# MLP down products with the activations stationary, and the MLP's split weights in other pools

## The chip, the cores and the metric

The kernel runs on one core of one Trainium2 chip. The metric is the device time of one execution in microseconds; runs of a kernel are compared by their median. A core has TensorE (PE in the profile; its weight loads are listed as PEld), VectorE (DVE), ScalarE (ACT), GpSimd (POOL) and SyncE (SP), which here issues all DMAs. "Granted clock" is the share of TensorE's full clock that the throttle allowed.

## The reference

One sequence of 256 tokens, width 2048, two layers. The first is an RWKV-7 layer, the second a forgetting-attention layer; after each stands the same MLP:

```python
def squared_relu_mlp(h, w_up, w_down):
    return jnp.square(jax.nn.relu(h @ w_up)) @ w_down
...
        x = x + mixed
        x = x + squared_relu_mlp(rms_norm(x, ffn_norm[layer]), mlp_w_up[layer], mlp_w_down[layer])
    return rms_norm(x, final_norm)
```

`w_up` is 2048 x 8192 and `w_down` 8192 x 2048 in each layer, all in float32: 64 MB each, 256 MB for both layers. All weights of the model are read once from HBM.

## The kernel before, in words

**Layout.** The stream `xT` lies in SBUF turned: 128 partitions hold 128 of the 2048 channels, 16 k-tiles, 256 tokens along the free side. An operand of a product (`opA`, `opB`) has for each k-tile two 256-column halves: a high part rounded to the type fp32r, and the rest, the low part. A weight block is treated in the same way: `load_split` (line 194 on) loads a raw block (tile `wr`, line 196), ScalarE casts it to the high part `wh` (line 204), and VectorE subtracts to get the low part `wl` (line 206). A product is high x high + high x low + low x high, three terms in fp32r. The other big products of the kernel (`gemm_steps`, line 216 on, matmuls in lines 212 to 214) do this with three 256-column matmuls for each 128x128 weight block; they load 256 rows x 512 columns at a time (512 KB) into the pool `wraw` (four buffers) and split k-tile by k-tile into `wsp` (five).

**The MLP before.** The hidden width of 8192 is taken in 4 chunks c of 2048. For each chunk come 4 up groups g of 512 columns, whose results become the operand `b`, and then 4 down groups of 512 columns. Both use `gemm_wide` (line 241 on). For each of 16 k-tiles and 4 weight blocks m of 128 columns, with the weight block stationary, there is one 512-column matmul, high weights against both halves of the activations (line 254), and one 256-column matmul, low weights against the high half (line 256). So lengths alternate: 512, 256, 512, 256. Each of the four m has one PSUM bank, [128, 512]; successive products take turns between the pool `psm` (4 banks, tag "mm") and the pool `pss` (4 banks, tag "side"), by the counter `wide`. At the end of a group ScalarE copies one half of each bank (line 261), VectorE adds the other (line 262), and `evac` goes on from there: for an up group relu (351), square on GpSimd (353) and the split into `b` (342, 343); for a down group the scaling by the norm's factor `r2` on VectorE (363) and the addition to `xT` on GpSimd (366, the last group of a layer on VectorE). Because relu and square let a positive factor through, the MLP's norm is not applied to its operand: `r2`, 1/mean-square by token, scales the down products. It is made after the first up group (`norm.ln`, line 324 with four matmuls against a matrix of ones, then two activations).

Loads are 512 rows x 512 columns (1024 KB, `WK` = 4 k-tiles) in three raw buffers of the MLP's own (`mraw0`, `mraw1`), splits are of two k-tiles at a time in three buffers each (`msp0`, `msp1`). In layer 0 the pools are opened in the order raw, split, other tiles; in layer 1 other tiles, raw, split.

**Around it.** Ahead of the MLP of layer 0 the last quarter of the time-mixing output projection runs (`gemm_group` with `w_o`), whose results are added to x (line 846) and at once scaled and split into the MLP's operand (lines 337 and 338). It uses two banks of `psm` per group. After the last chunk's down group, `final` is called for each pair of k-tiles: in layer 0 it makes squares for the next norm and the operand of the key/value product, in layer 1 squares for the final norm (306, 312) and the scaling by the final gain (1026); then come the final norm and the output DMAs. After layer 0's MLP come the forget-gate product (tile `zp`, in the pool `pss`), the key product (`gemm_steps`) and the value product, lines 920 to 931. The value product is written the other way round: the activations are stationary, 128 tokens at a time, and 512 columns of split weights are streamed (lines 929 to 931, tile `mmv`), so that its result lies with the tokens on the partitions; lines 932 and 933 scale it by token.

**Order.** The kernel is written in the Tile framework, whose scheduler places the instructions on each engine's queue, mostly in the order of the code, but not always: a few MLP matmuls, splits and loads stand in the queues among those of the projection before it. Each engine, and SP's queue of DMAs, goes through its queue in order. A tile with `bufs=n` takes n buffers in turn, and an instruction that writes a buffer waits until the last reader of its earlier content is through.

Of the kernel before, what the change touches and what calls it, by code (L numbers as in the profile page):

```python
# [10 lines left out]
F32 = mybir.dt.float32  # L11
F32R = mybir.dt.float32r
F16 = mybir.dt.float16
AF = mybir.ActivationFunctionType
ALU = mybir.AluOpType
# [3 lines left out]
P = 128  # L19
T = 256  # L20
D = 2048
# [7 lines left out]
RMS_EPS = 1e-6  # L29
CDEC = math.exp(-0.5)  # L30
NEG = -1.0e30
WK, WRAW, WSP = 4, 3, 3

VEC = ["mix0", "mix1", "ffn0", "ffn1", "fin", "kvn", "xm0", "xm1", "xm2", "xm3", "xm4", "xm5",
       "w0", "a0", "kk", "ka", "rk", "lnw", "lnb"]
# [84 lines left out]
def trunk_kernel(ctx: ExitStack, tc: tile.TileContext, xin, vecs, bfv, c32, c16, w_rkv, w1, w2, a1, a2, g1, g2,  # L120
# [64 lines left out]
    def side(name):  # L185
        return pss.tile([P, 512], F32, tag="side", name=name)

    def bcast(ap, n):
        return ap[:, None, :].to_broadcast([ap.shape[0], n, ap.shape[1]])
# [46 lines left out]
            for b in range(2):  # L236
                evac(b, ps[b])

    wide = {"n": 0}

    def gemm_wide(w, col, x, name, pool, wpools, evac):


        wide["n"] += 1
        ps = [(psm if wide["n"] % 2 else pss).tile([P, 512], F32, tag="mm" if wide["n"] % 2 else "side", name="mmw")
              for _ in range(4)]
        for k0 in range(0, KT, WK):
            hl = load_split(w[k0 * P:(k0 + WK) * P, col:col + 512].rearrange("(k p) n -> p k n", p=P), P, WK, 512, 2,
                            *wpools)
            for kk in range(WK):  # L250
                k = k0 + kk
                h, lo = hl[kk]
                for m in range(4):
                    mm(ps[m], h[:, m * P:(m + 1) * P], x[:, k].rearrange("p h t -> p (h t)"), start=k == 0, stop=False,  # L254
                       skip_group_check=True)
                    mm(ps[m][:, 0:T], lo[:, m * P:(m + 1) * P], x[:, k, 0, :], start=False, stop=k == KT - 1,  # L256
                       skip_group_check=True)
        for b in range(2):
            t = pool.tile([P, 2, T], F32, tag=name, name=name, bufs=3)
            for j in range(2):  # L260
                nc.scalar.copy(t[:, j, :], ps[2 * b + j][:, T:2 * T])
                V.tensor_tensor(t[:, j, :], ps[2 * b + j][:, 0:T], t[:, j, :], op=ALU.add)
            evac(b, t)
# [80 lines left out]


    def mlp(layer, norm, pool, wpools, a, b, final):
        r2 = None
        for c in range(FF // D):
            for g in range(4):
                def up_evac(i, t, g=g):  # L350
                    act(t, t, AF.Relu)  # L351
                    s = pool.tile([P, 2, T], F32, tag="ms", name="ms", bufs=3)
                    G.tensor_tensor(s, t, t, op=ALU.mult)  # L353
                    k = 4 * g + 2 * i
                    split(s, b[:, k:k + 2, 0, :], b[:, k:k + 2, 1, :])
                gemm_wide(w_up[layer], c * D + g * 512, a, "mt", pool, wpools, up_evac)
                if r2 is None:
                    norm.ln()
                    r2 = norm.power(-1.0, "nr2")
            for g in range(4):  # L360
                def down_evac(i, t, g=g, c=c):
                    k = 4 * g + 2 * i
                    V.tensor_tensor(t, t, bcast(r2, 2), op=ALU.mult)  # L363
                    xs = xT[:, k:k + 2, :]
                    end = c == FF // D - 1
                    (V if end and g == 3 else G).tensor_tensor(xs, xs, t, op=ALU.add)  # L366
                    if end:
                        final(2 * g + i)
                gemm_wide(w_down[layer, c * D:(c + 1) * D, :], g * 512, b, "mt", pool, wpools, down_evac)


    HA, HB = slice(0, 64), slice(64, 128)
# [493 lines left out]
    def after0(kp):  # L866
        norm2.add(kp)
        operand("kvn", kp, opBH, opBL)
    with tc.tile_pool(name="mraw0", bufs=WRAW, reuse_waits="tile") as mr, \
            tc.tile_pool(name="msp0", bufs=WSP, reuse_waits="tile") as ms, \  # L870
            tc.tile_pool(name="mlp0", bufs=2, reuse_waits="tile") as mp:
        for g in range(4):
            gemm_group(w_o, 512 * g, opAH, opAL, o_evac_for(g), range(12, 16), po[g] if g < 2 else None)
        mlp(0, norm, mp, (mr, ms), opB, opA, after0)


    s_c = dpool.tile([HEADS, T], F32, name="s_c")
# [138 lines left out]


    norm4 = Norm(npool, "n3")
    with tc.tile_pool(name="mlp1", bufs=2, reuse_waits="tile") as mp, \
            tc.tile_pool(name="mraw1", bufs=WRAW, reuse_waits="tile") as mr, \  # L1020
            tc.tile_pool(name="msp1", bufs=WSP, reuse_waits="tile") as ms:

        def after1(kp):
            norm4.add(kp, kp >= KT // 2 - 2)
            for k in (2 * kp, 2 * kp + 1):
                act(xT[:, k, :], xT[:, k, :], AF.Copy, scale=vcol("fin", k))
        mlp(1, norm3, mp, (mr, ms), opA, opB, after1)
        norm4.ln()
        rf = norm4.power(-0.5, "nrf")
        osrc = out.rearrange("(k p) t -> p k t", p=P)  # L1030
        for kp in range(KT // 2):
            xs = xT[:, 2 * kp:2 * kp + 2, :]
            (G if kp in (1, 5) else V).tensor_tensor(xs, xs, bcast(rf, 2), op=ALU.mult)
            dma(osrc[:, 2 * kp:2 * kp + 2, :], xs)
# [53 lines left out]
```

## Time and profile before

| | |
|---|---|
| time, median of 3 runs | 2511.7 us (2502.09, 2511.7, 2518.87) |
| the profiled execution's own time | 2515.21 us |
| its span, first to last instruction | 2513.4 us |
| mean granted clock | 0.993 |
| TensorE, VectorE, ScalarE, GpSimd busy | 98%, 63%, 51%, 13% |
| DMA queue, share of 16 engines | 57.1% |
| read from HBM, written | 445.44 MB, 24.13 MB, 187 GB/s over the span |
| MLP of layer 0, first to last matmul of tile mmw | 649.6 to 1383.8 us |
| MLP of layer 1 | 1783.7 to 2495.1 us |

How to read the lines below. A group of instructions is given as: line, engine, operation, output tile <- input tiles, shapes, count | busy us, mean ns of one | idle time of the engine before them and what ended it. A row by stretches of time has: the stretch, its length, then for PE, PEld, DVE, ACT and POOL the busy time and in brackets the number of instructions (where the view is of one line alone, only the engines that the line uses), then granted clock, mean share of the DMA engines, GB/s. A row by time has the start, the duration, engine, line, operation and, in square brackets, the wait before it and who ended it. A row by tile has the shortest, median and longest duration in ns and the first and last start. A row by waits has who waited for whom, total us, times, longest. Matmuls are pipelined: their durations overlap, and the distance between starts is what one costs.

### The profile page before, as it was taken

What the parts mean: (1) busy time and instruction counts of PE and PEld (TensorE: products, weight loads), DVE (VectorE), ACT (ScalarE), POOL (GpSimd) and SP (SyncE); (2) the same over time, 40 slices, a digit from 0 to 9 for tenths busy, and PEclk for the clock granted to TensorE, in tenths of its full rate; (3) what the DMA queues carried; (4) which work ended last, traced back from release to release, by engine and by line L of the source; (5) the groups of instructions that cost most, each with busy time, mean ns of one, the idle gap of its engine ahead of it and who ended that gap; (6) DMA issues with size and microseconds to landing.
All of it is one profiled execution on the core that took longest, in us unless ns stands there. A gap on an engine that the chain in (4) does not pass through costs nothing.

```text
span 2513.4 us, 49132 instructions
## 1 busy us (share of the span) xinstructions
PE 2454.1 (98%) x20214; PEld 2198.8 (87%) x20214; DVE 1592.7 (63%) x2329; ACT 1270.8 (51%) x2072; POOL 325.2 (13%) x272
## 2 busy tenths in 40 slices
PE   7999999999999999999999999999999999999997
PEld 6999988789888888888888998999988888888886
DVE  7986677766755555555557655677555555555555
ACT  3866545454554454444445444555454454544554
POOL 1000001001311112112112100110112102112112
PEclk9999999999999999999999999999999999999998
DMA  5777865554755555555553456546355555655653
GB/s 162 237 247 244 266 206 161 180 169 152 262 188 185 185 185 187 187 190 188 179 192 135 149 185 193 174 164 228 131 185 189 195 187 188 194 188 187 195 188 118
DMA packets 274017, 472.76 MB, mean 188 GB/s; under 512 B 43248, under 2 KB 53760, under 8 KB 273792
## 3 DMA queue, kind: packets, MB, share of 16 engines
q1 hardware_dynamic: 273792, 469.62, 57.1%
q8 instruction: 158, 2.59, 0.4%
q14 instruction: 67, 0.55, 0.1%
HBM read 445.44 MB, written 24.13 MB: 187 GB/s over the span
## 4 chain that ended last, share of the span: by engine, by line
PE 90%; DVE 5%; DMA 3%; ACT 1%; issue 1%; DVEq 0%; SPq 0%; ACTq 0%
PE mmw L254 38%; PE mmw L256 19%; PE mm L212 7%; PE mm L214 7%; PE mm L213 7%; PE zyus L778 1%; PE i L609 1%; PE mmv L929 1%; PE mmv L930 1%; PE mmv L931 1%; DVE wl L206 1%; PE lps L473 1%; DMA k<-s_k 1%; DMA wr<-in_mlp_w_up_dram 1%; PE mmg L508 1%
## 5 line engine op out<-in xcount | busy, mean ns | idle before, releaser
L206 DVE TENSOR_TENSOR wl<-wr,wh 128x1024 fp32r<-128x1024 f32 (+1 forms) x1013 | 975.7, 967 | 747.0 <-ACT wh L204 740.2
L204 ACT CAST wh<-wr 128x512 fp32r<-128x512 f32 (+1 forms) x1011 | 841.4, 837 | 910.3 <-PE mmw L254 594.9
L254 PE MATMUL mmw<-opB,wh 128*128 128x512 f32 x2048 | 717.4, 396 | 5.1 <-DVE xT L846 5.1
L254 PE MATMUL mmw<-opA,wh 128*128 128x512 f32 x2048 | 718.0, 396 | 0.2 <-ACT wh L204 0.2
L256 PE MATMUL mmw<-opA,wl 128*128 128x256 f32 x2048 | 571.6, 279 | 0.9 <-DVE wl L206 0.9
L256 PE MATMUL mmw<-opB,wl 128*128 128x256 f32 x2048 | 570.8, 279 | 0.0
L254 PEld LDWEIGHTS mmw<-opB,wh 128*128 128x128 f32 x2048 | 384.4, 188 | 97.7 <-DVE xT L846 5.3
L254 PEld LDWEIGHTS mmw<-opA,wh 128*128 128x128 f32 x2048 | 384.4, 188 | 93.3 <-ACT wh L204 0.5
L256 PEld LDWEIGHTS mmw<-opA,wl 128*128 128x128 f32 x2048 | 385.7, 188 | 1.4 <-DVE wl L206 1.3
L256 PEld LDWEIGHTS mmw<-opB,wl 128*128 128x128 f32 x2048 | 385.6, 188 | 0.2
L212 PE MATMUL mm<-opB,wh 128*128 128x256 f32 x1024 | 298.7, 293 | 0.4 <-ACT opB L342 0.3
L213 PE MATMUL mm<-opB,wh 128*128 128x256 f32 x1024 | 292.9, 286 | 1.5 <-DVE opB L343 0.7
L214 PE MATMUL mm<-opB,wl 128*128 128x256 f32 x1024 | 291.9, 286 | 1.6 <-DVE wl L206 1.6
L212 PE MATMUL mm<-opA,wh 128*128 128x256 f32 x768 | 227.1, 296 | 0.2 <-ACT wh L204 0.2
L214 PE MATMUL mm<-opA,wl 128*128 128x256 f32 x768 | 218.3, 284 | 0.6 <-DVE wl L206 0.5
L213 PE MATMUL mm<-opA,wh 128*128 128x256 f32 x768 | 217.9, 284 | 0.0
L213 PEld LDWEIGHTS mm<-opB,wh 128*128 128x128 f32 x1024 | 197.1, 193 | 4.9 <-DVE opB L343 2.0
L212 PEld LDWEIGHTS mm<-opB,wh 128*128 128x128 f32 x1024 | 196.5, 192 | 5.5 <-ACT opB L342 2.1
L214 PEld LDWEIGHTS mm<-opB,wl 128*128 128x128 f32 x1024 | 196.7, 192 | 2.9 <-DVE wl L206 2.1
L366 POOL TENSOR_TENSOR xT<-xT,mt 128x512 f32<-128x512 f32 x60 | 128.8, 2146 | 533.8 <-DVE mt L363 533.8
L353 POOL TENSOR_TENSOR ms<-mt 128x512 f32<-128x512 f32 x64 | 81.1, 1267 | 636.5 <-ACT mt L351 636.5
L212 PEld LDWEIGHTS mm<-opA,wh 128*128 128x128 f32 x768 | 147.5, 192 | 3.1 <-ACT wh L204 0.4
(259 smaller groups left out, 2499.9 us busy)
## 6 DMA issues: line engine op xcount, KB each, us to landing
wr<-in_mlp_w_up_dram SPq DMA_DIRECT2D x128, 1024.0 KB, 5.4
wr<-in_mlp_w_down_dram SPq DMA_DIRECT2D x128, 1024.0 KB, 5.0
wr<-in_w_rkv_dram SPq DMA_DIRECT2D x96, 512.0 KB, 4.7
wr<-in_w_kvf_dram SPq DMA_DIRECT2D x64, 512.0 KB, 3.6
wr<-in_w_o_dram SPq DMA_DIRECT2D x32, 512.0 KB, 4.1
wr<-in_fox_w_q_dram SPq DMA_DIRECT2D x32, 512.0 KB, 3.5
wr<-in_fox_w_o_dram SPq DMA_DIRECT2D x32, 512.0 KB, 3.8
wr<-in_g_dram SPq DMA_DIRECT2D x8, 512.0 KB, 4.1
```

Of the source, the lines that this page charges most:

```text
L204: nc.scalar.copy(h, raw[:, k:k + per, :])
L206: (G if share["l"] and c % share["l"] == 0 else V).tensor_tensor(lo, raw[:, k:k + per, :], h.bitcast(F32), op=ALU.subtract)
L212: mm(ps, wh, xh, start=first and bank_first, stop=False, skip_group_check=True)
L213: mm(ps, wh, xl, start=False, stop=False, skip_group_check=True)
L214: mm(ps, wl, xh, start=False, stop=last, skip_group_check=True)
L254: mm(ps[m], h[:, m * P:(m + 1) * P], x[:, k].rearrange("p h t -> p (h t)"), start=k == 0, stop=False, skip_group_check=True)
L256: mm(ps[m][:, 0:T], lo[:, m * P:(m + 1) * P], x[:, k, 0, :], start=False, stop=k == KT - 1, skip_group_check=True)
L353: G.tensor_tensor(s, t, t, op=ALU.mult)
L366: (V if end and g == 3 else G).tensor_tensor(xs, xs, t, op=ALU.add)
L473: mm(ps[0:c1 - c0, m, :], raw[:, kk, c0:c1], xs, start=k == 0 and m == 0, stop=k == KT - 1, skip_group_check=True)
L508: mm(ps[:, m, :], raw[:, kk, c:c + P], gh[:, kk, :], start=kk == 0 and m == 0, stop=kk == 1, skip_group_check=True)
L609: mm(ps[hs, c, :], lhs[hs, c, :], rhs[hs, c, :] if len(rhs.shape) == 3 else rhs[hs], start=start, stop=True, skip_group_check=True)
```

## The change

- `WK` goes from 4 to 2 (loads of 512 KB), the MLP's own raw pools go, and the loads use `wraw`, the pool of the other products. `WSP` goes from 3 to 4. The split pool is opened first, the pool of the other tiles after it, in both layers.
- The up products stay in `gemm_wide`; for two k-tiles there are now eight 512-column matmuls, then eight 256-column ones. The counter `wide` begins at 1, so that the first product takes `pss`.
- The down products go to the new `down_group`: the activations are stationary (128 tokens i, high or low part), 512 columns of split weights are streamed, three matmuls for each k-tile and i. The result lies with the tokens on the partitions, in one bank for each i. It is scaled by token (`rc`) and gathered over the four chunks in an SBUF tile `y` [128, 2, 2048]: the first chunk by ScalarE, the others by one VectorE pass each. For the last two k-tiles all of i = 0 comes before i = 1.
- In the last chunk `finish(g)` turns `y` back: eight 128x128 transposes on TensorE in two tiles `ytp`, and VectorE adds them to `xT`; then `final`. It is called for group g after the first two k-tiles of group g + 1, for the last group at the end.
- `norm.ln` comes after the second up group, and after the fourth `r2` is turned into the column `rc` by two transposes and a copy.

```diff
-WK, WRAW, WSP = 4, 3, 3
+WK, WSP = 2, 4
...
-    wide = {"n": 0}
+    wide = {"n": 1}
...
-            for kk in range(WK):
-                k = k0 + kk
-                h, lo = hl[kk]
-                for m in range(4):
-                    mm(ps[m], h[:, m * P:(m + 1) * P], x[:, k].rearrange("p h t -> p (h t)"), start=k == 0, stop=False,
-                       skip_group_check=True)
-                    mm(ps[m][:, 0:T], lo[:, m * P:(m + 1) * P], x[:, k, 0, :], start=False, stop=k == KT - 1,
-                       skip_group_check=True)
+            for k1 in range(0, WK, 2):
+                ks = [(k0 + k1 + i, *hl[k1 + i]) for i in range(2)]
+                for k, h, _ in ks:
+                    for m in range(4):
+                        mm(ps[m], h[:, m * P:(m + 1) * P], x[:, k].rearrange("p h t -> p (h t)"), start=k == 0,
+                           stop=False, skip_group_check=True)
+                for k, _, lo in ks:
+                    for m in range(4):
+                        mm(ps[m][:, 0:T], lo[:, m * P:(m + 1) * P], x[:, k, 0, :], start=False, stop=k == KT - 1,
+                           skip_group_check=True)
...
     def mlp(layer, norm, pool, wpools, a, b, final):
-        r2 = None
+        y = pool.tile([P, 2, D], F32, tag="y", name="y", bufs=1)
+        late = []
+
+        def down_group(c, g):
+
+            pool_, tag = ((pss, "side"), (psm, "mm"))[g // 2]
+            ps = [pool_.tile([P, 512], F32, tag=tag, name="mmd") for _ in range(2)]
+            for k0 in range(0, KT, WK):
+                r0 = c * D + k0 * P
+                hl = load_split(w_down[layer, r0:r0 + WK * P, g * 512:g * 512 + 512]
+                                .rearrange("(k p) n -> p k n", p=P), P, WK, 512, 2, *wpools)
+                last = k0 + WK == KT
+                for i, kk in [(i, kk) for i in range(2) for kk in range(WK)] if last else \
+                        [(i, kk) for kk in range(WK) for i in range(2)]:
+                    k, t = k0 + kk, slice(i * P, (i + 1) * P)
+                    h, lo = hl[kk]
+                    mm(ps[i], b[:, k, 0, t], h, start=k == 0, stop=False)
+                    mm(ps[i], b[:, k, 1, t], h, start=False, stop=False)
+                    mm(ps[i], b[:, k, 0, t], lo, start=False, stop=k == KT - 1)
+                    if last and kk == WK - 1:
+                        yg = y[:, i, g * 512:g * 512 + 512]
+                        if c == 0:
+                            act(yg, ps[i], AF.Copy, scale=rc[:, i:i + 1])
+                        else:
+                            V.scalar_tensor_tensor(yg, ps[i], rc[:, i:i + 1], yg, op0=ALU.mult, op1=ALU.add)
+                if k0 == 0 and late:
+                    finish(late.pop())
+
+        def finish(g):
+
+            for j in range(2):
+                kp = 2 * g + j
+                tp = side("ytp").rearrange("p (k t) -> p k t", k=2)
+                for kk in range(2):
+                    for i in range(2):
+                        n = (2 * kp + kk) * P
+                        nc.tensor.transpose(tp[:, kk, i * P:(i + 1) * P], y[:, i, n:n + P], C("ident"))
+                xs = xT[:, 2 * kp:2 * kp + 2, :]
+                V.tensor_tensor(xs, tp, xs, op=ALU.add)
+                final(kp)
+
...
-                if r2 is None:
+                if c == 0 and g == 1:
                     norm.ln()
                     r2 = norm.power(-1.0, "nr2")
+                if c == 0 and g == 3:
+                    rps = side("rc")
+                    for i in range(2):
+                        nc.tensor.transpose(rps[:, i * P:(i + 1) * P], r2[:, i * P:(i + 1) * P], C("ident"))
+                    rc = pool.tile([P, 2], F32, tag="rc", name="rc", bufs=1)
+                    V.tensor_copy(rc, rps.rearrange("p (i n) -> p i n", n=P)[:, 0:2, 0])
             for g in range(4):
-                def down_evac(i, t, g=g, c=c):
-                    k = 4 * g + 2 * i
-                    V.tensor_tensor(t, t, bcast(r2, 2), op=ALU.mult)
-                    xs = xT[:, k:k + 2, :]
-                    end = c == FF // D - 1
-                    (V if end and g == 3 else G).tensor_tensor(xs, xs, t, op=ALU.add)
-                    if end:
-                        final(2 * g + i)
-                gemm_wide(w_down[layer, c * D:(c + 1) * D, :], g * 512, b, "mt", pool, wpools, down_evac)
+                down_group(c, g)
+                if c == FF // D - 1:
+                    late.append(g)
+        finish(late.pop())
...
-    with tc.tile_pool(name="mraw0", bufs=WRAW, reuse_waits="tile") as mr, \
-            tc.tile_pool(name="msp0", bufs=WSP, reuse_waits="tile") as ms, \
+    with tc.tile_pool(name="msp0", bufs=WSP, reuse_waits="tile") as ms, \
             tc.tile_pool(name="mlp0", bufs=2, reuse_waits="tile") as mp:
...
-        mlp(0, norm, mp, (mr, ms), opB, opA, after0)
+        mlp(0, norm, mp, (wraw, ms), opB, opA, after0)
...
-    with tc.tile_pool(name="mlp1", bufs=2, reuse_waits="tile") as mp, \
-            tc.tile_pool(name="mraw1", bufs=WRAW, reuse_waits="tile") as mr, \
-            tc.tile_pool(name="msp1", bufs=WSP, reuse_waits="tile") as ms:
+    with tc.tile_pool(name="msp1", bufs=WSP, reuse_waits="tile") as ms, \
+            tc.tile_pool(name="mlp1", bufs=2, reuse_waits="tile") as mp:
...
-        mlp(1, norm3, mp, (mr, ms), opA, opB, after1)
+        mlp(1, norm3, mp, (wraw, ms), opA, opB, after1)
```

## The prediction

> **What bounds the kernel now.** I read first the page: busy times, the chain that ended last, the costliest groups.
>
> ```profile
> PE 2454.1 (98%) x20214; PEld 2198.8 (87%) x20214; DVE 1592.7 (63%) x2329; ACT 1270.8 (51%) x2072; POOL 325.2 (13%) x272
> PE 90%; DVE 5%; DMA 3%; ACT 1%; issue 1%; DVEq 0%; SPq 0%; ACTq 0%
> L254 PE MATMUL mmw<-opB,wh 128*128 128x512 f32 x2048 | 717.4, 396 | 5.1 <-DVE xT L846 5.1
> L256 PE MATMUL mmw<-opA,wl 128*128 128x256 f32 x2048 | 571.6, 279 | 0.9 <-DVE wl L206 0.9
> ```
>
> TensorE ends 90% of the chain, and the wide products of the two MLPs (tile mmw, two lines, 4096 matmuls each) are most of it. The 396 and 279 ns are latencies that overlap; what counts is the distance from one start to the next. For that I took stretches in which TensorE never waits and divided their length by the matmuls in them: the two MLPs, the key product (256 columns only) and the value product (512 columns only, activations stationary, the form that the change gives the down products), with the instructions of all engines, and then line 254 alone.
>
> ```profile
> 1415.00:1480.00 65.00, 65.00 (x544) 65.00 (x544) 34.47 (x52) 28.06 (x46) 0.00 (x0) 1.00 0.59 184
> 1490.00:1570.00 80.00, 80.00 (x354) 66.24 (x354) 42.78 (x62) 38.32 (x62) 0.00 (x0) 1.00 0.62 195
> 700.00:1300.00 600.00, 600.00 (x1699) 319.05 (x1698) 1.00 0.56 186
> 1850.00:2450.00 600.00, 600.00 (x1732) 324.53 (x1731) 1.00 0.57 190
> 659.00:676.00 17.00, 16.86 (x50) 9.07 (x49) 1.00 0.68 230
> ```
>
> The first bracket is matmuls; one is cut by the edge, so I divide by one less. A 256-column matmul takes 65/543 = 119.7, say 120 ns; a 512-column one 80/353 = 226.6 ns. The difference of 256 columns is 106.6 ns, so each matmul carries about 13.4 ns that do not depend on its length. A pair of 512 and 256 columns would be 346.6 ns. The MLP of layer 1 runs at that: 600/1731 = 346.6. The MLP of layer 0 runs at 600/1698 = 353.4, 6.8 ns more per pair, at a granted clock of 1.00 in both and with no idle time. It is not the layer as such: in its first microseconds (last row) layer 0 too runs at 17/49 = 346.9, and the longer step begins after the norm's matmuls cut into the stream. So the alternation of lengths can run in a good and in a poor rhythm; a stream of one length shows only one.
>
> **The change part by part.**
>
> *Down products with activations stationary.* Per k-tile and 512-column group four pairs become six 512-column matmuls: the same 3072 columns, two matmuls fewer. Before: 4 x 353.4 = 1413.6 ns in layer 0, 4 x 346.6 = 1386.4 in layer 1. After, by the value product: 6 x 226.6 = 1359.6. There are 256 such steps per layer (4 chunks, 4 groups, 16 k): layer 0 saves 256 x 54.0 = 13.8 us, layer 1 256 x 26.8 = 6.9 us.
>
> *Up products by length.* Eight 512-column matmuls, then eight 256-column ones: 226.6 + 120 = 346.6 per pair. Layer 0 saves 1024 x 6.8 = 7.0 us, layer 1 nothing. Matmuls together: 27.7 us. Bounds: if the poor rhythm stays in all up products, 27.7 - 2 x 7.0 = 13.7; no row gives a step under 119.7 or 226.6.
>
> *Transposes.* The accumulated y is turned back by 32 transposes per layer, plus 2 for the norm. The attention has such transposes, three at a time:
>
> ```profile
> 1718.05 0.28 PE L214 MATMUL mm<-opB,wl 128*128 128x256 f32 x1
> 1718.17 0.49 PE L968 MATMUL ptp<-k,lg 128*128 128x128 f32 x3
> 1718.42 0.36 PE L212 MATMUL mm<-opB,wh 128*128 128x256 f32 x1
> L968 PE MATMUL ptp<-k,lg x48: 270/271/272, 1601.8 to 1718.4; 128*128 128x128 f32 x48
> ```
>
> From 1718.17 to 1718.42 three pass, 83 ns each, though one lasts 271. 68 x 83 = 5.6 us. Upper bound, if each costs its whole duration: 68 x 271 = 18.4. I take 5.6, since they come eight in a row. The Trainium skill ("TensorE: Matmul & The Clock Gate", Part 4: PE-mode transpose) gives some 275 ns for a transpose inside a kernel, and warns of this path; the 271 of the last row agrees as a duration, the 83 does not agree as a price. By the page alone the sum would rise by about 13 us.
>
> *Evacuation.* Per down group four ScalarE copies, four VectorE adds, two scalings and two GpSimd adds go; two scaled passes over 128x512 come, on ScalarE in the first chunk, then on VectorE.
>
> ```profile
> L262 DVE TENSOR_TENSOR mt<-mmw,mt 128x256 f32<-128x256 f32 x256 | 99.0, 421 | 9.8 <-ACT mt L261 9.5
> L363 DVE TENSOR_TENSOR mt<-mt,nr 128x512 f32<-128x512 f32 x64 | 62.6, 978 | 1.0
> L338 DVE SCALAR_TENSOR_TENSOR opB<-xT,vec,opB 128x256 fp32r<-128x256 f32 x32 | 28.2, 925 | 3.6 <-ACT opB L337 3.6
> L933 DVE TENSOR_SCALAR vS<-mmv,rT x4: 749/750/752, 1507.3 to 1572.5; 128x512 f32<-128x512 f32 x4
> 1122.48 1.05 ACT L204 CAST wh<-wr 128x1024 fp32r<-128x1024 f32 x1 [1.72 <-PE mmw L254]
> 1123.56 1.23 DVE L206 TENSOR_TENSOR wl<-wr,wh 128x1024 fp32r<-128x1024 f32 x1 [1.54 <-ACT wh L204]
> ```
>
> VectorE loses 4 x 0.42 + 2 x 0.98 = 3.6 us per group; the new pass is not shown, and lies between the 0.75 us of line 933 (same shape, from PSUM) and 1.85 (two of line 338's 925 ns); I take the near row, 1.5 us for two. In steady state both engines wait for TensorE (last two rows), so this costs nothing on the path. What it could cost is at three points per layer: the transposes of group g stand in TensorE's queue after the first two k-tiles of group g+1, 12 x 0.227 = 2.7 us behind the end of g. By then VectorE must have done a split that stands in front (1.23) and two passes (1.5): just 2.7. Matmuls of group g+1 queue behind a late transpose. Bounds 0 to 6 us (six points, none late or each a whole split and more late); I take 1.
>
> *Loads.* 256 loads of 1024 KB become 512 of 512 KB into the four buffers that the other products use; raw depth falls from 12 to 8 k-tiles, split depth rises from 6 to 8.
>
> ```profile
> wr<-in_mlp_w_up_dram SPq DMA_DIRECT2D x128, 1024.0 KB, 5.4
> wr<-in_w_kvf_dram SPq DMA_DIRECT2D x64, 512.0 KB, 3.6
> DMA to landing us min/median/max: 4.7/6.1/8.0
> ```
>
> A load serves two k-tiles, 2.72 us of TensorE. A raw buffer comes round after four of these, 10.9 us, of which cast and subtraction take 1.05 + 1.23 and the issue 0.4: 8.2 us are left for a median landing of 3.6. Even the crowded start of layer 0 (the last row, the landings issued between 645 and 675 us) stays under. The value product takes 512 KB per 12 x 226.6 ns already, at 195 GB/s, and TensorE has no idle time there. Cost nothing; without this cover, see the slower rival.
>
> *Start of layer 0.* The first up product of layer 0 takes the PSUM banks that the output projection still holds; the change makes it start on the other four.
>
> ```profile
> 644.28 0.28 PE L213 MATMUL mm<-opA,wh 128*128 128x256 f32 x1
> 649.62 0.80 PE L254 MATMUL mmw<-opB,wh 128*128 128x512 f32 x1 [5.06 <-DVE xT L846]
> 650.21 0.41 PE L256 MATMUL mmw<-opB,wl 128*128 128x256 f32 x1
> ...
> 653.84 0.41 PE L214 MATMUL mm<-opA,wl 128*128 128x256 f32 x1
> 644.88 2.29 DVE L206 TENSOR_TENSOR wl<-wr,wh 128x1024 fp32r<-128x1024 f32 x1
> 647.09 1.87 DVE L338 SCALAR_TENSOR_TENSOR opB<-xT,vec,opB 128x256 fp32r<-128x256 f32 x2
> 648.88 0.68 DVE L846 TENSOR_TENSOR xT<-mm,xr 128x512 f32<-128x512 f32 x1
> 649.49 0.67 DVE L206 TENSOR_TENSOR wl<-wr,wh 128x512 fp32r<-128x512 f32 x1
> ```
>
> TensorE waits 5.2 us for line 846 to clear the banks, then runs slow matmuls (410 ns): from 650.21 to 653.84 there are 17 steps, 213 instead of 120 ns each, 1.6 us. The whole is about 7 us. But VectorE is full here: what is late next is line 206 for the last group of the projection (649.49), behind operands of the earlier groups. What surely leaves its queue is the MLP's early split of 2.29 us, which now comes after the projection's loads. I take 3, bounds 0 and 7.
>
> *Small ones.* In layer 1 the projection waits once for a split that stands behind an early MLP split, and the MLP of layer 0 once:
>
> ```profile
> PE mm L214 <- DVE wl L206: 1.0, 1, 1.0
> PE mmw L256 <- DVE wl L206: 0.9, 1, 0.9
> ```
>
> With loads in one order and two more k-tiles split ahead I take 1.5 of these 1.9 us as gone (bounds 0 and 1.9). The moved norm issues the same four matmuls and two activations, later, behind a product rather than ahead of it: nothing.
>
> *The two ends.* The last group now ends with pass, transposes, add. At the end of the kernel today:
>
> ```profile
> 2494.88 0.40 PE L254 MATMUL mmw<-opB,wh 128*128 128x512 f32 x1
> 2495.11 0.28 PE L256 MATMUL mmw<-opB,wl 128*128 128x256 f32 x1
> 2497.54 0.63 ACT L306 ACTIVATE nsq<-xT 128x512 f32<-128x512 f32 x1 [1.74 <-DVE xT L366]
> 2499.02 0.61 ACT L306 ACTIVATE nsq<-xT 128x512 f32<-128x512 f32 x1
> ```
>
> From the last matmul's end (2495.39) to the first square 2.15 us, to the second 3.63. After: second pass 0.75, three transposes and the latency of one 0.5, add 0.68, some 0.15 of handing over: 2.1; the second square follows ScalarE's two scalings as now, 3.5. Nothing at both ends (bounds -1 and +1).
>
> **Sum**, against the profiled execution's own 2515.2 us (span 2513.4): -27.7 + 5.6 + 1 - 3 - 1.5 = -25.6, which gives 2489.6; I say 2489. That execution lies 3.5 us above the median of 2511.7, and one with layer 0 in the good rhythm too would lie 13.9 lower (2048 x 6.8), near the lowest of the runs, 2502.1. Against the median the forecast is 0.9% less.
>
> **The rivals.**
>
> *The rhythm, not the length.* What makes 353.4 of 346.6 has no row. The pools of the split weights lie in a different order in the two layers, and if their place decided, a new place could bring either step, in the 512-column stream too. For: two layers with the same instructions differ by 2%. Against: layer 0 changes its step without changing its place, and the value product steps evenly. If the up products stay at 353.4 in both layers: 2489 + 13.9 = 2503.
>
> *Transposes at their full price, or late passes.* 18.4 - 5.6 = 12.8 and up to 5 of waiting: 2489 + 15 = 2504. For: TensorE takes its queue in order, and slack is nil by my count. Against: 83 ns measured, and VectorE is less loaded than before.
>
> *The start becomes clean.* If the scheduler puts the last splits ahead of the operands, the whole 7 us go: 2485.
>
> *Slower: loads late.* Place: the raw buffers, four of 512 KB. Point: a landing time above 8.2 us as a rule. From there every microsecond more delays each round of four loads by one, 128 rounds: with landings of 9 us, 0.8 x 128 = 102 us more, 2591. For: less raw data ahead, twice the issues; the 8.0 of the crowded start touches the point. Against: 3.6 us where 512 KB loads run steadily. The Trainium skill ("DMA: Bandwidth & Descriptors", Rules for kernel authors) asks for at least 1 MiB per DMA for the highest bandwidth, which speaks against halving the loads; here the trace does not agree, since 195 GB/s with 512 KB stand against 186 and 190 with 1024.
>
> **How the numbers follow.** Forecast 0.53 (own range 2483 to 2496), rhythm 0.13, transposes and late passes 0.12, clean start 0.16, late loads 0.06. About 1%, 25 us, is what a measurement of this kernel can tell from no change; faster by that means below 2486.6. The clean start gives 0.14 of it and the lower half of the forecast 0.27: 0.41. Slower by 1% comes from late loads only: 0.06. The rest, 0.53, is within 1%. The range: all gains at their bounds give 2515.2 - 27.7 + 5.6 - 7 - 1.9 - 1 = 2483, and I go to 2480 for what I may have missed; above, it takes in the two rivals at 2503 and 2504, with 2 us to spare: 2506.
>
> **What would show it.** Right: line of the down product 226 to 228 ns from start to start, in both layers; the up product 346.6 per pair in both; ytp transposes under 100 ns apart; PE's wait for line 846 gone. Wrong: idle time of TensorE before a line of the down products, named to a split (late loads, if the split waits for a DMA) or to the pass over y; a step over 230 ns in the 512-column stream; more than 350 per pair in the up products.

## The result, and the profile after

| | before | after |
|---|---|---|
| median of 6 runs | 2509.84 us (2499.87 to 2518.87) | 2489.68 us (2485.85 to 2493.76) |
| profiled execution: time, span | 2515.21, 2513.4 us | 2485.85, 2483.8 us |
| MLP of layer 0, first to last matmul | 734.2 us | 711.8 us |
| MLP of layer 1 | 711.4 us | 709.5 us |

The ratio on record is 0.9923, with a 95% interval of 0.9896 to 0.9951 (the two medians divided give 0.9920): 0.8% faster, the case "within 1%" of the prediction, 0.7 us above its 2489. Between the two profiled executions lie 29.4 us, more than between the medians: that of before is high among its runs, that of after the lowest.

The page of after:

```profile
PE 2433.0 (98%) x19258; PEld 2158.7 (87%) x19258; DVE 1527.2 (61%) x2199; ACT 1240.0 (50%) x1960; POOL 193.4 (8%) x212
PE 91%; DVE 4%; DMA 2%; ACT 1%; issue 1%; DVEq 0%; SPq 0%; ACTq 0%
L254 PE MATMUL mmw<-opA,wh 128*128 128x512 f32 x1024 | 256.7, 392 | 0.0
L365 PE MATMUL mmd<-wh,opA 128*128 128x512 f32 x512 | 199.6, 390 | 0.0
wr<-in_mlp_w_up_dram SPq DMA_DIRECT2D x256, 512.0 KB, 3.7
```

TensorE still ends 91% of the chain, with no idle time ahead of the two MLP lines shown. So the chunks can be measured from edge to edge. The rows by time of TensorE at the edges of the second chunk in layer 0 and in layer 1 (an up part begins at line 254, a down part at 365):

```profile
825.46 0.62 PE L254 MATMUL mmw<-opB,wh 128*128 128x512 f32 x2
914.82 0.40 PE L365 MATMUL mmd<-wh,opA 128*128 128x512 f32 x1
1001.89 0.62 PE L254 MATMUL mmw<-opB,wh 128*128 128x512 f32 x2
...
1933.64 0.62 PE L254 MATMUL mmw<-opA,wh 128*128 128x512 f32 x2
2023.00 0.40 PE L365 MATMUL mmd<-wh,opB 128*128 128x512 f32 x1
2110.07 0.61 PE L254 MATMUL mmw<-opA,wh 128*128 128x512 f32 x2
```

Down, 384 matmuls in 87.07 us: 226.7 ns each, in both layers, as predicted. Up, 256 pairs in 89.36 us: 349.1 ns per pair in both layers, not 346.6.

The start of layer 0, by rows by time: VectorE's first addition after the projection, and the 65th 512-column matmul of the up product, which in both kernels follows 64 pairs. Before:

```profile
631.82 0.68 DVE L846 TENSOR_TENSOR xT<-mm,xr 128x512 f32<-128x512 f32 x1
681.04 0.59 PE L254 MATMUL mmw<-opB,wh 128*128 128x512 f32 x1
```

After, with TensorE's only wait for an MLP operand, from the view of the waits:

```profile
627.98 0.68 DVE L889 TENSOR_TENSOR xT<-mm,xr 128x512 f32<-128x512 f32 x1
670.14 2.00 PE L254 MATMUL mmw<-opB,wh 128*128 128x512 f32 x8
```

```profile
PE mmw L258 <- DVE wl L206: 1.8, 2, 1.4
```

49.22 us became 42.16: 7.1 us less, of which some 0.6 are the norm's four matmuls, which now come later. The wait for the addition is gone, and with it the slow matmuls behind it: in before the granted clock is 0.50 from 650.3 to 653.8 us, in after it is 1.00 all through this start. And the addition itself came 3.8 us earlier, before anything that the change touches; in the profiles of this study with four raw buffers, of whatever kernel, it lies between 628 and 635 us, and in a second profile of after at 630.8. That part is chance, and the traces show where it arose: from 394 to 399 us and from 469 to 478 us, in stages that the change leaves alone, the mean granted clock is 0.66 and 0.62 in before and 1.00 in after, and across these two stretches before falls about 5 us behind after (a little comes back later).

Eight transposes between down products, by time:

```profile
1291.96 0.40 PE L367 MATMUL mmd<-wl,opA 128*128 128x512 f32 x1
1292.19 1.03 PE L385 MATMUL ytp<-k,y 128*128 128x128 f32 x8
1292.98 0.47 PE L365 MATMUL mmd<-wh,opA 128*128 128x512 f32 x1
1293.30 0.39 PE L366 MATMUL mmd<-wh,opA 128*128 128x512 f32 x1
```

They start 0.79/8 = 99 ns apart; with the longer first step behind them (0.32 instead of 0.227) they cost (1.34 - 2 x 0.227)/8 = 111 ns each. No wait stands before them. The end of the kernel:

```profile
2464.51 0.75 DVE L373 SCALAR_TENSOR_TENSOR y<-mmd,rc,y 128x512 f32<-128x512 f32 x1 [7.43 <-PE mmd L367]
...
2465.44 0.39 PE L367 MATMUL mmd<-wl,opB 128*128 128x512 f32 x1
...
2468.07 0.63 ACT L308 ACTIVATE nsq<-xT 128x512 f32<-128x512 f32 x1 [12.25 <-DVE xT L387]
...
2469.54 0.61 ACT L308 ACTIVATE nsq<-xT 128x512 f32<-128x512 f32 x1
```

The pass over y takes the 0.75 us that were taken from line 933. From the last matmul's end (2465.83) it is 2.24 us to the first square and 3.71 to the second; 2.15 and 3.63 before.

### The profile page after: what moved, and what is told of

Same layout as the page of the kernel before. It is cut to its first block, busy times and chain, and to the rows that moved or that the text cites. A ratio compares the mean times of both kernels' runs of the same rounds, so it can differ in the third digit from the quotient of the medians.

```text
span 2483.8 us, 47527 instructions
## 1 busy us (share of the span) xinstructions
PE 2433.0 (98%) x19258; PEld 2158.7 (87%) x19258; DVE 1527.2 (61%) x2199; ACT 1240.0 (50%) x1960; POOL 193.4 (8%) x212
## 4 chain that ended last, share of the span: by engine, by line
PE 91%; DVE 4%; DMA 2%; ACT 1%; issue 1%; DVEq 0%; SPq 0%; ACTq 0%
PE mmw L254 19%; PE mmw L258 10%; PE mmd L365 9%; PE mmd L366 9%; PE mmd L367 9%; PE mm L212 8%; PE mm L213 7%; PE mm L214 7%; PE zyus L821 1%; PE mmv L971 1%; PE mmv L973 1%; PE mmv L972 1%; PE i L652 1%; DVE wl L206 1%; PE lps L516 1%
## 5 line engine op out<-in xcount | busy, mean ns | idle before, releaser
L206 DVE TENSOR_TENSOR wl<-wr,wh 128x512 fp32r<-128x512 f32 (+1 forms) x1013 | 971.0, 964 | 782.0 <-ACT wh L204 773.3
L204 ACT CAST wh<-wr 128x1024 fp32r<-128x1024 f32 (+2 forms) x1011 | 840.6, 837 | 983.6 <-PE mmd L366 344.3
L254 PE MATMUL mmw<-opA,wh 128*128 128x512 f32 x1024 | 256.7, 392 | 0.0
L254 PE MATMUL mmw<-opB,wh 128*128 128x512 f32 x1024 | 256.7, 392 | 0.0
L254 PEld LDWEIGHTS mmw<-opA,wh 128*128 128x128 f32 x1024 | 184.3, 189 | 33.4 <-ACT nln L328 0.3
L254 PEld LDWEIGHTS mmw<-opB,wh 128*128 128x128 f32 x1024 | 184.3, 189 | 33.4 <-ACT nln L328 0.3
L365 PE MATMUL mmd<-wh,opB 128*128 128x512 f32 x512 | 199.6, 390 | 0.0
L365 PE MATMUL mmd<-wh,opA 128*128 128x512 f32 x512 | 199.6, 390 | 0.0
L367 PE MATMUL mmd<-wl,opB 128*128 128x512 f32 x512 | 199.2, 389 | 0.0
L367 PE MATMUL mmd<-wl,opA 128*128 128x512 f32 x512 | 199.2, 389 | 0.0
L366 PE MATMUL mmd<-wh,opA 128*128 128x512 f32 x512 | 199.2, 389 | 0.0
L366 PE MATMUL mmd<-wh,opB 128*128 128x512 f32 x512 | 199.2, 389 | 0.0
```

Of the source, the lines that this page charges most:

```text
L204: nc.scalar.copy(h, raw[:, k:k + per, :])
L206: (G if share["l"] and c % share["l"] == 0 else V).tensor_tensor(lo, raw[:, k:k + per, :], h.bitcast(F32), op=ALU.subtract)
L365: mm(ps[i], b[:, k, 0, t], h, start=k == 0, stop=False)
L366: mm(ps[i], b[:, k, 1, t], h, start=False, stop=False)
L367: mm(ps[i], b[:, k, 0, t], lo, start=False, stop=k == KT - 1)
```

## The experiments

The theory: the matmuls' own steps (length and order) make nearly all of the gain, and the rest comes at the start. Its rivals: the place of the buffers makes the two rhythms of before; the counter gains more than the start shows; transposes and loads cost more than they seem to. Where one time is given, it is that of a single execution. Executions of one kernel differ by 8 us (after) to 20 us (before), so these runs are read stage by stage rather than by their totals.

**Down products alone.** After, with the up products alternating as before.

```diff
-            for k1 in range(0, WK, 2):
-                ks = [(k0 + k1 + i, *hl[k1 + i]) for i in range(2)]
-                for k, h, _ in ks:
-                    for m in range(4):
-                        mm(ps[m], h[:, m * P:(m + 1) * P], ...
-                for k, _, lo in ks:
-                    for m in range(4):
-                        mm(ps[m][:, 0:T], lo[:, m * P:(m + 1) * P], ...
+            for kk in range(WK):
+                k = k0 + kk
+                h, lo = hl[kk]
+                for m in range(4):
+                    mm(ps[m], h[:, m * P:(m + 1) * P], ...
+                    mm(ps[m][:, 0:T], lo[:, m * P:(m + 1) * P], ...
```

> The changed kernel with the up products alternating again (512, 256, 512, 256). Theory, a fixed cost per matmul and a rhythm that history sets: the down stretches stay at 87.1 us per chunk (384 x 226.7 ns); the up pairs, 349.1 ns in the changed kernel, go to 346.6 or to 353.4 in either layer, free of the place of the split pools, so 1024 x -2.5 to 1024 x +4.3 = -2.5 to +4.4 us per layer. Rival, the place decides: the split pools lie at the same place in both layers now, so both layers show the same step, and it stays for a whole layer.

Measured: 2499.68 us. The 512-column up matmuls by tile, with first and last start: in the first chunk of each layer behind the norm's matmuls, and in the second chunk of each layer.

```profile
L254 PE MATMUL mmw<-opB,wh x123: 392/392/395, 701.2 to 743.5; 128*128 128x512 f32 x123
L254 PE MATMUL mmw<-opA,wh x123: 392/392/395, 1813.0 to 1855.2; 128*128 128x512 f32 x123
...
L254 PE MATMUL mmw<-opB,wh x256: 389/398/403, 831.2 to 921.2; 128*128 128x512 f32 x128
L254 PE MATMUL mmw<-opA,wh x256: 389/398/403, 1942.9 to 2033.0; 128*128 128x512 f32 x128
```

42.3/122 = 346.7 ns per pair in the one stretch, 90.0/255 = 353 in the other, both steps in both layers, with the same buffers. What stands between is an interruption: the norm's four matmuls end the poor rhythm, and behind each stretch of down products it is there again. So the step goes with the stream's history, not with the place of the pools. Down chunks took 87.07 us as in after. The MLPs took 715.9 and 713.0 us, 4.1 and 3.5 more than in after: that is what grouping by length is worth beside the new down products.

**Length alone.** Before, with the products of both parts grouped by length (the diff above turned round, in the kernel before); one profile, and then several runs.

> The kernel before with nothing but the order by length in the wide products, up and down. Theory: the order ends the two rhythms, 349 ns per pair in both layers: layer 0 gains 2048 x 4.3 = 8.8 us against the profiled run of before, layer 1 loses 2048 x 2.5 = 5.1 us; in sum about 2511 us as profiled there (2515.2 - 3.7). Rival, the place decides the step: layer 0 stays at 353 and layer 1 at 347, as before.

> The kernel before with the products of both MLP parts grouped by length and nothing else changed, timed over several executions. Its one profile showed 349.1 to 349.6 ns per pair in both layers, so no rhythm that an interruption can shift. The executions of the kernel before spread over 18 us (2499.65 to 2517.65), those of the kernel after over 8 us (2485.85 to 2493.76). If the wide spread of the kernel before is its rhythm (2 x 1024 pairs at 346.7 or 353.3 ns, 6.8 us per 1024 of them), the executions of this kernel lie within about 9 us of each other, around 2508 us, and none reaches the 2500 to 2503 us of the kernel before's fastest. Rival: the spread comes from the stages ahead of the MLP or from the chip, and this kernel's executions spread over 15 us or more as well.

One execution: 2511.01 us. Then 2509.23 us, the median of 12 runs (2505.28 to 2514.41) beside 2512.13 of before (16 runs, 2497.94 to 2518.04), ratio 0.9998, interval 0.9979 to 1.0017. Line 254 by stretches:

```profile
700.00:1300.00 600.00, 430.12 (x1720) 308.87 (x1719) 1.00 0.57 188
1850.00:2450.00 600.00, 430.11 (x1719) 308.92 (x1718) 1.00 0.57 188
```

600/1719 = 349.0 ns per pair in both layers: against the profiled before a gain in layer 0 and a loss in layer 1. So grouping alone gains nothing that can be measured. But it narrows the spread: 9 us over 12 runs, and none of them under 2505, where 5 of before's 16 lie; the standard deviations are 2.6 and 6.7 us. The wide spread of before then probably comes mostly from its rhythm. The 33 times of before in its three series of runs bear this out: 10 lie between 2497.9 and 2504.8 us, 23 between 2508.0 and 2518.9, and the means of the two groups are 12.5 us apart, where layer 0 in the good rhythm would save 13.9. It is not shown, since no execution of before under 2505 us has been profiled.

**Before again**, unchanged.

> The kernel before, unchanged, profiled once more. Theory, history sets the rhythm: the step of a layer may differ from the first profile (353.4 in layer 0, 346.6 in layer 1), and within a layer it changes only after an interruption of the stream. Rival, the place of the tiles decides: 353.4 and 346.6 again.

```profile
700.00:1300.00 600.00, 600.00 (x1699) 319.08 (x1699) 1.00 0.56 186
1850.00:2450.00 600.00, 600.00 (x1732) 324.52 (x1731) 1.00 0.58 190
```

2516.93 us, with the same steps of 353.4 and 346.6 in the same stretches as in the first profile. This is what the rival expected, and the theory allowed it too, so this run does not tell them apart; the run with the down products alone does.

**Transposes twice.**

```diff
-                        nc.tensor.transpose(tp[:, kk, i * P:(i + 1) * P], y[:, i, n:n + P], C("ident"))
+                        for _ in range(2):
+                            nc.tensor.transpose(tp[:, kk, i * P:(i + 1) * P], y[:, i, n:n + P], C("ident"))
```

> The changed kernel with each of the 64 transposes of y issued twice into the same place. My price, 83 ns each: the stretches of the last chunk's down groups grow by 24 x 83 ns = 2.0 us per layer, the whole by 5.3 us or less, since the last eight of a layer stand in a chain that waits anyway. Rival, the full duration of 271 ns each: 6.5 us per stretch, 17 us in all.

2498.73 us, but its first addition lies 6.7 us later than in after, so the stage itself is compared: the last down part of layer 0, up to the last group's transposes. With doubled transposes, and then in after:

```profile
1274.22 0.40 PE L365 MATMUL mmd<-wh,opA 128*128 128x512 f32 x1
...
1366.67 0.60 PE L386 MATMUL ytp<-k,y 128*128 128x128 f32 x4
```

```profile
1267.67 0.40 PE L365 MATMUL mmd<-wh,opA 128*128 128x512 f32 x1
...
1357.50 0.38 PE L385 MATMUL ytp<-k,y 128*128 128x128 f32 x2
```

92.45 against 89.83 us: 2.62 for 24 more transposes, 109 ns each. The first 24 cost (89.83 - 87.07)/24 = 115 ns each, against a down part without any. The 83 ns were too low by a quarter, the 271 far too high.

**The first bank.** After, with the counter at its old value.

```diff
-    wide = {"n": 1}
+    wide = {"n": 0}
```

> The changed kernel with the counter of the wide products at 0 again, so that the first up product takes the banks that the output projection holds. From the first addition after the projection to the first relu of the MLP take 49.6 us in the kernel before and 45.2 in the changed one. Theory, the banks: most of the 4.4 us come back, with a wait of TensorE of some 5 us for the addition to xT ahead of the first up matmul. Rival, the order of the loads and splits gave the gain: it stays at 45 us.

2520.05 us, one execution, above every recorded time of before. From the view of the waits, and a stretch with all engines:

```profile
PE mmd L365 <- DVE mt L264: 10.7, 6, 1.8
PE mmw L254 <- DVE xT L889: 6.5, 1, 6.5
...
PE rc L405 <- DVE mt L264: 3.6, 2, 1.8
```

```profile
1109.30:1112.00 2.70, 2.70 (x8) 2.11 (x7) 1.55 (x2) 1.60 (x3) 1.31 (x2) 0.50 0.28 100
```

The start is back: 6.5 us of waiting for the addition, and from the first addition to the 65th matmul 48.8 us, against 42.2 in after and 49.2 in before. To the first relu it takes 51.8 us, so 6.6 us came back where most of 4.4 was expected. The rest had not been foreseen. With the counter at 0 the fourth up group and the first down group of a chunk stand in the same four banks of `pss`, and TensorE waits 1.8 us for the evacuation (line 264) at each of the eight changes from up to down. After four of these waits, one in layer 0 and three in layer 1, the granted clock falls to 0.50 for about 3.4 us. MLP of layer 1: 723.8 us against 709.5; of the 14.3 more, 9.0 lie in the up parts, counted to the next down matmul and so with the waits, and 5.1 in the three down parts that begin at half the clock. So the one line of the counter carries the start, and 14 us in layer 1.

**Blocks of one and of four k-tiles.** The up products with blocks of 4 + 4 and of 16 + 16 matmuls (8 + 8 in after); for four k-tiles two loads are split ahead of a block.

```diff
-            for k1 in range(0, WK, 2):
-                ks = [(k0 + k1 + i, *hl[k1 + i]) for i in range(2)]
+        for k0 in range(0, KT, 2 * WK):
+            hl = []
+            for r0 in (k0, k0 + WK):
+                hl += load_split(w[r0 * P:(r0 + WK) * P, ...
+            ks = [(k0 + i, *hl[i]) for i in range(2 * WK)]
```

> The changed kernel with the up products in blocks of one k-tile: four matmuls of 512 columns, four of 256. In the changed kernel a block of 8 + 8 takes 2793 ns, 19 more than 8 x 226.7 + 8 x 120. Theory, the loss comes once per change from short to long: 19 ns per 8 matmuls, 351.4 ns per pair, 89.96 us per chunk's up products instead of 89.36. Rival, the loss belongs to the 512-column matmul with stationary weights: the same 349.1 per pair; third, the rhythm: 346.7 or 353.3.

> The changed kernel with the up products in blocks of four k-tiles: sixteen matmuls of 512 columns, sixteen of 256, over two loads. Theory, once per change: 19 ns per 32 matmuls, 347.9 ns per pair, 89.05 us per chunk instead of 89.36, 2.5 us less over both layers. Rival, the loss belongs to the matmul: 349.1. What could spoil it: a block holds two of the four split buffers to its end, so that splits come later; then waits of TensorE for a split show in the up products.

2490.55 and 2488.02 us. The edges of the second up part, for one k-tile and then for four:

```profile
827.61 0.39 PE L254 MATMUL mmw<-opB,wh 128*128 128x512 f32 x1
...
917.40 0.40 PE L364 MATMUL mmd<-wh,opA 128*128 128x512 f32 x1
```

```profile
829.96 0.62 PE L255 MATMUL mmw<-opB,wh 128*128 128x512 f32 x2
...
919.00 0.40 PE L366 MATMUL mmd<-wh,opA 128*128 128x512 f32 x1
```

89.79 and 89.04 us: 350.7 and 347.8 ns per pair, where once per change would give 351.4 and 347.9 and the rival 349.1. What lies above 346.7 is 4 x 4.0 = 16 ns per block of one k-tile, 8 x 2.4 = 19 of two, 16 x 1.1 = 18 of four: a nearly fixed price for each block. The starts in after show where it is paid: behind a run of 256-column matmuls the first five distances of 512 columns are 233, 236, 228, 232 and 231 ns instead of 227, 27 ns more in all; behind the change back, the first distance of 256 columns is 113 instead of 120. The price is not that of every change from short to long, though: the alternating order has one in each pair, and runs at 346.7 or 353.4.

**Two raw buffers.** After, with half the depth of raw data.

```diff
-    wraw = ctx.enter_context(tc.tile_pool(name="wraw", bufs=4))
+    wraw = ctx.enter_context(tc.tile_pool(name="wraw", bufs=2))
```

> The changed kernel with two raw weight buffers instead of four, for every product. Theory, the point of the slower rival: a buffer's round is landing 3.7 + issue 0.4 + cast 1.05 + subtraction 1.23 = 6.4 us for two loads, 3.2 per load, where TensorE needs 2.72 (down) and 2.79 (up); so the MLPs become bound by loads, 256 x 0.45 = 115 us more per layer, TensorE waits for splits and those for DMAs. Rival, the loads are hidden at any depth: no change.

2782.62 us. Waits, one down part by tile, and a stretch over the MLP of layer 0, against the like stretch of after:

```profile
PE mmw L254 <- ACT wh L204: 53.8, 104, 2.3
PE mmd L365 <- ACT wh L204: 26.4, 34, 2.2
...
L365 PE MATMUL mmd<-wh,opA x128: 387/389/501, 1021.3 to 1121.1; 128*128 128x512 f32 x128
...
720.00:1420.00 700.00, 656.72 (x3165) 523.03 (x3166) 325.10 (x332) 289.37 (x352) 34.53 (x31) 1.00 0.54 166
```

```profile
700.00:1340.00 640.00, 640.00 (x3242) 546.22 (x3241) 347.83 (x355) 301.71 (x369) 39.16 (x32) 1.00 0.60 191
```

TensorE's waits name the cast (line 204), and the cast itself waits for the MLP's loads, 431.3 us in all for `w_down` and 338.6 for `w_up`. Line 365 starts once in three down matmuls, 99.8/127 = 0.786 us apart; a load serves four such steps, 3.14 us. Two buffers then come round in 6.3 us, which is the sum that the prediction made for one round: landing 3.6 + 1.05 + 1.23 + 0.4 = 6.3. With four buffers the limit is 10.9 us for the same 6.3, and there TensorE has no idle time in 640 us. The MLPs take 816.3 and 815.5 us, 105 and 106 more than in after, where 115 were expected; what the whole time has grown by beyond that lies in the other products, which use the same pool. So with four buffers the loads are hidden. That there the late-loads rival would need landings above 8.2 us as a rule is worked out, not run.

**After and blocks of four again, and the key product in the wide form.** The last kernel has blocks of four k-tiles in the up products and makes the key product, which had three 256-column matmuls per weight block, by `gemm_wide`. With that, two small transposes for the value product move ahead of the key product, and the counter takes an extra step before and after it. In part:

```diff
-            def k_ev(b, ps, g=g):
+            def k_ev(b, t, g=g):
                 m = 4 * g + 2 * b
-                V.tensor_tensor(kT[:, m:m + 2, :], ps, bcast(rkv, 2), op=ALU.mult)
-            gemm_group(w_kvf, 512 * g, opBH, opBL, k_ev)
+                V.tensor_tensor(kT[:, m:m + 2, :], t, bcast(rkv, 2), op=ALU.mult)
+            gemm_wide(w_kvf, 512 * g, opB, "qT", fp, (), k_ev, 5)
```

> The kernel after, unchanged, as the yardstick of the two kernels beside it: 2485 to 2494 us, and 0.992 of the kernel before. The first addition after the projection will lie anywhere from 627 to 635 us by what earlier runs of all kernels showed; up chunks 89.4 us, down chunks 87.1 us.

> Blocks of four k-tiles in the up products, timed. The one profile gave 89.04 us per up chunk against 89.36: 8 x 0.32 = 2.6 us under the kernel after, if the place in the profile carries over to the medians; if the spread between executions, some 10 us, hides it, the interval holds 1.

> Blocks of four k-tiles in the up products, as in the run before, and the key product (256 steps of three 256-long matmuls, 3 x 120 = 360 ns) turned into the same 512 + 256 form, in blocks of two k-tiles. If the fixed part of about 13.4 ns of each matmul is what the wide form saves, the key steps go from 360 ns to the 349.1 ns that blocks of two gave in the up products: 256 x 10.9 = 2.8 us less between the gate product and the value product, and the whole kernel about 2.5 us (blocks of four) + 2.8 us = 5 us under the kernel after. Rival: the evacuation of a wide group (two copies, two adds and a product instead of one product) or the order of the tiles holds TensorE at the groups' ends, and the stretch is not shorter.

The ratios are those on record; the medians divided give 0.9904, 0.9904 and 0.9883.

| | median of 6 runs | ratio to before (2512.09, 11 runs) |
|---|---|---|
| after | 2487.95 us (2486.22 to 2492.66) | 0.9916 (0.9892 to 0.9940) |
| blocks of four | 2487.87 us (2483.42 to 2492.15) | 0.9912 (0.9886 to 0.9939) |
| blocks of four, key product wide | 2482.72 us (2478.33 to 2488.15) | 0.9894 (0.9869 to 0.9919) |

The forget-gate product's first and the value product's first matmul, by tile, in the last kernel and then in after:

```profile
L212 PE MATMUL zp<-opB,wh x16: 276/278/362, 1357.3 to 1364.0; 128*16 128x256 f32 x16
...
L974 PE MATMUL mmv<-wh,opB x128: 389/389/396, 1455.6 to 1542.0; 128*128 128x512 f32 x128
```

```profile
L212 PE MATMUL zp<-opB,wh x16: 276/276/362, 1357.6 to 1364.4; 128*16 128x256 f32 x16
...
L971 PE MATMUL mmv<-wh,opB x128: 389/389/476, 1458.6 to 1545.1; 128*128 128x512 f32 x128
```

98.3 against 101.0 us, 2.7 less where 2.8 was expected. Blocks of four gain 0.32 us per up chunk in the profile, 2.6 in all, but by the medians nothing; the last kernel lies 5.2 us under after in the same measurement (their runs overlap between 2486.2 and 2488.2), and it is the fastest of all.

## Why the prediction came out right

The total was right in part by luck: errors of both signs stood in it, and cancelled. The up products gained 5.1 us less than the sum had, the start 3.5 and the late passes 1 more. It is luck too that the median lies within 0.7 us of 2489: the sum started from an execution 5.4 us above the median of before, and the medians fell by 20.2 us (24.1 when measured again), not by 25.6. Against the profiled executions:

| term | predicted | measured | from |
|---|---|---|---|
| down products | -13.8, -6.9 | -13.5, -6.7 | 4 x 87.07 against 1024 x 353.3 and 346.7 |
| up products | -7.0, 0 | -4.3, +2.4 | 4 x 89.36 against the same |
| transposes | +5.6 | +5.9 | 52 between other matmuls, at 113 ns; the other 16 lie in the ends |
| late passes | +1 | 0 | no wait |
| start of layer 0 | -3 | -6.5 | 49.2 to 42.2, less 0.6 moved |
| small waits | -1.5 | -1.9 | the two are gone; 1.8 of new ones lie in the start |
| ends | 0 | 0 | 2.24 and 3.71 us |
| ahead of the change | | -3.8 | first addition, chance |
| sum | -25.6 | -28.4 | 29.6 in the spans; of the other 1.2, 1.0 is shorter waiting in the forget-gate product (1.5 to 0.5) |

**Down products**: right, in size and in both layers. The value product had shown the step, and this stream of one length shows the same step in every chunk of every kernel here that has four raw buffers, as long as the clock stays at 1.00.

**Up products**: the mis-sized step is "226.6 + 120 = 346.6 per pair". Each block costs 16 to 19 ns more than that, paid behind the change from short to long, and a block of eight pairs has one such change. That is 2.4 ns per pair, 5 us in all. The 349.1 lies between the prediction's sign of being right (346.6) and that of being wrong (over 350). The prediction had taken both numbers from streams that never change their length and put them together. Its rival, "the rhythm, not the length", fell with the profile of after, where neither layer shows 353.4.

**Start**: "I take 3, bounds 0 and 7". Nearly the upper bound came: its rival, the clean start, was the better account. The matmuls of 410 ns that the prediction counted with it stand at a granted clock of 0.50, and without the wait the clock stays at 1.00. What was to stand in the way, the last group's split behind the operands of earlier groups, left 1.8 us of waits, already within the 6.5. What the counter does later, keeping the last up group and the first down group in different pools, the prediction did not see at all; it got this right for no reason of its own. The run with the counter at 0 shows its price.

**Transposes**: the row with three at a time gave 83 ns, the eight cost 109 to 115. The Trainium skill ("TensorE: Matmul & The Clock Gate", Part 4: PE-mode transpose) gives some 275 ns for a 128x128 transpose in bf16 within a kernel; a float32 one lasts about as long here (271 ns), but that is not what one more costs.

**Loads**: nothing, as predicted. The Trainium skill ("DMA: Bandwidth & Descriptors", Rules for kernel authors) asks for at least 1 MiB per DMA; here 512 KB loads ran at 191 GB/s without making TensorE wait, so the rule has no bearing on this kernel's time. Nor did the rates that the prediction compared, 195 against 186 and 190 GB/s, speak against the rule: TensorE had no idle time in those stretches, so they are the rates at which it took the weights. The depth does count: with two buffers it is some 105 us per layer.

**The runs of before**: the prediction's remark that an execution with layer 0 in the good rhythm would lie near the lowest run is supported by the narrow spread of the grouped form and by the two groups of times of before, not shown by a profile.

## What to carry to other kernels

Measure a matmul's price as the distance between starts in a stream of the very order that you plan, since a change of length, and even the stream's history, moves it by 1 to 2%. When a product changes the banks it uses, write down which banks the neighbours hold at each change of stage, not only at the first one. Before comparing two profiles, look where they differ ahead of the change: here 3.8 us of the 29.6 did.

## What the hardware showed that was not expected

A stream that alternates 512 and 256 columns runs at 346.7 or at 353.3 ns per pair with the same instructions and buffers. The norm's four matmuls in between were enough to switch it: from 346.9 to 353.4 in layer 0 of before, from 353.5 to 346.7 in layer 1 of before and in both layers of the kernel with the down products alone. Which state of TensorE this is stays open, as does what the 16 to 19 ns per block are. The two orders differ in more than length: the alternating one writes each PSUM bank twice in a row, the grouped one changes the bank with every matmul. No run separates the two.

The granted clock fell to 0.50 for some 3.4 us after a wait of 1.8 us, in four of eight such waits, in the kernel with the counter at 0. The Trainium skill ("TensorE: Matmul & The Clock Gate", Why this matters for your kernels) advises to avoid gaps over about 3 us; here shorter ones were enough, though not each time.
